# One layer of a Hymba trunk on one core: the sums of a pair of weight tiles made in place, one more buffer of split weights, and one of the pair's sums added by a DMA

## The chip, the cores and the metric

The kernel runs on one core of a Trainium2 chip. The metric is the time of one execution in microseconds of the device. Each time is a median of runs on one chip; a profile comes from one execution of its own. The engines are TensorE (PE; its weight loads are PEld), VectorE (DVE), ScalarE (ACT), GpSimd (POOL) and SyncE (SP); SP and ACT issue plain loads, POOL the DMAs that add.

## The reference, cut to what matters

```
S = 256, D = 2048, F = 5632, float32
x = x + 0.5 * swiglu(rmsnorm(x), wg1, wu1, wd1)      # FFN 1
x = x + mixing(rmsnorm(x))                           # attention and mLSTM heads, projections
x = x + 0.5 * swiglu(rmsnorm(x), wg2, wu2, wd2)      # FFN 2
out = rmsnorm(x)
swiglu(h, wg, wu, wd) = (silu(h @ wg) * (h @ wu)) @ wd
```

The two FFNs make up most of the work: each multiplies 256 rows with two weights of 2048 x 5632 (gate and up) and one of 5632 x 2048 (down), all in float32.

## The kernel before, in words

**Float32 out of three products.** TensorE gets each operand as a high part and a low part. `split` (L112 to L114) makes them: ScalarE casts the source to the high part (L113), VectorE subtracts that from the source for the low part (L114). `mm3` (L139 to L143) then issues three matmuls per product of 128 x 128 by 128 x 512: high by high (L141), high by low (L142), low by high (L143).

**The FFN.** Gate and up have 11 column chunks of 512. They are worked off in parts of 3, 3, 3 and 2 chunks; c = 0, 1, 2 is a chunk's place in its part. After each part the down projection multiplies that part's rows of the hidden state, in two steps of two column chunks each, and its results are scaled on ScalarE (`part`, L281) and added to x by an accumulating DMA from GpSimd (L282). A chunk's gate result goes through Silu on ScalarE (`sg`, L309).

**Paired.** One `Paired` (L322 on) multiplies the activations with two weights at once, `wa` and `wb`: gate and up of a chunk, or two chunks of down. Its first `ns` pairs of k-tiles (4 for gate and up, 2 in one chunk, 3 for down and 1 in the last part) go by a scheme with seven products for eight, out of sums of tiles; the remaining k-tiles go as plain units of two k-tiles each (`plain`). The raw tile of a pair has four rows of 128 x 512: a0 and a1 of wa, b0 and b1 of wb. The sums of weights are T1 = a0 + b0, b0 + b1, T2 = a0 + b0 + b1 and T4 = T2 + a1.

- `first` makes, for each pair, the split tile f (T1 and b0 + b1) and the split tile e (a0 and T2), and multiplies both into the banks p5, p7 (f) and p1, p6 (e) of PSUM. After the split of e, a DMA from GpSimd adds a1 to T2 in the raw tile (L361), which makes T4.
- `combine` mixes the four banks on ScalarE and VectorE (`u`, L368 to L373).
- `second` multiplies the tiles a1 and T4 (`bare`) and b1 (`upper`, two pairs in one split tile), and the plain units of wa. Its results leave two banks, which the caller takes (sg or part).
- `third` multiplies the plain units of wb. It is a generator: `Chain.run` puts its units between the pairs of the next Paired's `first`.

In all 122 pairs are worked off: 82 of gate and up, 40 of down.

**Buffers and order.** The pool `wr` has 4 raw tiles (`raw`), `wrp` has 5 raw buffers of two rows, for plain units (`rawp`) and for the sums (`sums`), `wsp` has 4 split tiles (high `wh`, low `wl`), and PSUM has 6 banks `acc` for products. A buffer is given out in the order in which tiles are asked for, so a split tile waits for the matmuls of the tile four back. The loads, sums and splits of weights are emitted at a priority that is 400 ahead (AHEAD); a scheduler puts the instructions of each engine in a fixed order from these priorities when the program is built, and each engine executes its own in that order. All loads of weights are issued by SP.

In `first` two loads of 512 KB bring a pair's raw tile (L347, issued in L166); VectorE makes T1 and b0 + b1 in a `sums` buffer with one operation of 1024 columns (L350) and T2 in the raw tile with one of 512 (L352); then f and e are split one behind the other.

Of the kernel before, what the change touches and what calls it, by code (L numbers as in the profile page):

```python
# [9 lines left out]
F32 = mybir.dt.float32  # L10
# [3 lines left out]
ALU = mybir.AluOpType  # L14
# [3 lines left out]
P = 128  # L18
# [6 lines left out]
CW = 512  # L25
# [7 lines left out]
UK = 2  # L33
# [4 lines left out]
LK = 4  # L38
AHEAD = 400
# [10 lines left out]
def tile_trunk_layer(ctx: ExitStack, tc: tile.TileContext, x, xt, par, bias_if, lamv, fnorm,  # L50
                     wg1, wu1, wd1, wqk0, wqk1, wqk2, win, wout, wg2, wu2, wd2, out):
    nc = tc.nc
# [2 lines left out]
    slots = ctx.enter_context(tc.tile_pool(name="slots", bufs=21))  # L55
    work = ctx.enter_context(tc.tile_pool(name="work", bufs=8))
    wr = ctx.enter_context(tc.tile_pool(name="wr", bufs=4))
    wrp = ctx.enter_context(tc.tile_pool(name="wrp", bufs=5))
    wsp = ctx.enter_context(tc.tile_pool(name="wsp", bufs=4))
    small = ctx.enter_context(tc.tile_pool(name="small", bufs=2))  # L60
    ps_acc = ctx.enter_context(tc.tile_pool(name="ps_acc", bufs=6, space=PSUM))
    ps_tr = ctx.enter_context(tc.tile_pool(name="ps_tr", bufs=2, space=PSUM))
# [4 lines left out]
    def nm(s):  # L67
        uid[0] += 1
        return f"{s}_{uid[0]}"
# [42 lines left out]
    def split(src, hi, lo):  # L112
        nc.scalar.copy(hi, src)  # L113
        nc.vector.tensor_tensor(out=lo, in0=src, in1=hi.bitcast(F32), op=ALU.subtract)  # L114

    def pair_tiles(pool, tag, shape):
        return (pool.tile(shape, F32R, tag=tag + "h", name=nm(tag + "h")),
                pool.tile(shape, F32R, tag=tag + "l", name=nm(tag + "l")))
# [43 lines left out]
            f()  # L162
        pending.clear()

    def load_pair(dst, w, k):
        nc.sync.dma_start(dst, w[k // LK][:, k % LK:k % LK + 2, :])  # L166

    def load_unit(w, k):
        raw = wrp.tile([P, UK, CW], F32, tag="rawp", name=nm("rawp"))
        with tc.high_priority(offset=AHEAD):  # L170
            load_pair(raw, w, k)
        return raw

    def units(accs, xp, w, nk, last_units=1, ahead=None, in_pieces=False, w0=0,
# [144 lines left out]
    def bank():  # L319
        return ps_acc.tile([P, CW], F32, tag="acc", name=nm("acc"))  # L320

    class Paired:  # L322
# [2 lines left out]

        def __init__(self, xp, wa, wb, nk, ns, w0=0):
            self.xp, self.wa, self.wb, self.k0 = xp, wa, wb, w0 * LK
            self.ns, self.rest = ns, range(2 * ns, nk, UK)  # L330
            self.raws = []

        def prod(self, acc, j, xi, w, wi, first, last, on=False):
            xh, xl = self.xp[j]
            mm3(acc, xh[:, xi, :], xl[:, xi, :], w[0][:, wi, :], w[1][:, wi, :], first, last, on)

        def first(self):


            self.p1, self.p6, self.p7, self.p5 = (bank() for _ in range(4))  # L340
            for j in range(self.ns):
                raw = wr.tile([P, 4, CW], F32, tag="raw", name=nm("raw"))
                self.raws.append(raw)
                at, end = j == 0, j == self.ns - 1
                with tc.high_priority(offset=AHEAD):
                    for i, w in enumerate((self.wa, self.wb)):
                        load_pair(raw[:, 2 * i:2 * i + 2, :], w, self.k0 + 2 * j)  # L347
                    f = pair_tiles(wsp, "w", [P, 2, CW])
                    sums = wrp.tile([P, 2, CW], F32, tag="rawp", name=nm("sums"))
                    nc.vector.tensor_tensor(out=sums, in0=raw[:, 0:4:3, :],  # L350
                                            in1=raw[:, 2:3, :].to_broadcast([P, 2, CW]), op=ALU.add)
                    nc.vector.tensor_tensor(out=raw[:, 2, :], in0=sums[:, 0, :], in1=raw[:, 3, :], op=ALU.add)  # L352
                    e = pair_tiles(wsp, "w", [P, 2, CW])
                    split(sums, *f)
                    split(raw[:, 0:3:2, :], *e)
                self.prod(self.p5, j, S1, f, 0, at, end)
                self.prod(self.p7, j, S3, f, 1, at, end)
                self.prod(self.p1, j, A1, e, 0, at, end)
                self.prod(self.p6, j, S2, e, 1, at, end)
                with tc.high_priority(offset=AHEAD):  # L360
                    nc.gpsimd.dma_start(raw[:, 2, :], raw[:, 1, :], accum_op=ALU.add)  # L361
                yield

        def combine(self):
# [21 lines left out]
        def second(self):  # L386

            n11, n21, n12 = self.p1, self.p7, self.p5

            def bare(j):  # L390
                with tc.high_priority(offset=AHEAD):
                    t = pair_tiles(wsp, "w", [P, 2, CW])
                    split(self.raws[j][:, 1:3, :], *t)
                self.prod(n11, j, A2, t, 0, False, False, True)
                self.prod(n21, j, B2, t, 1, False, False, True)

            def upper(j0):
                with tc.high_priority(offset=AHEAD):
                    t = pair_tiles(wsp, "w", [P, 2, CW])
                    js = range(j0, min(j0 + 2, self.ns))  # L400
                    for i, j in enumerate(js):
                        split(self.raws[j][:, 3, :], t[0][:, i, :], t[1][:, i, :])
                for i, j in enumerate(js):
                    self.prod(n12, j, S4, t, i, False, False, True)

            for i in range(max(self.ns, len(self.rest))):
                if i < self.ns:
                    bare(i)
                    if i % 2 or i == self.ns - 1:
                        upper(i - i % 2)  # L410
                if i < len(self.rest):
                    self.plain(self.wa, self.rest[i], (n11, n21))()
                if i == 0:
                    flush()
            return [n11, n21]
# [46 lines left out]
    def ffn(chain, xp, rstd, wg, wu, wd, finish, first=None):  # L462
# [20 lines left out]
        done = 0  # L483
        for part, (n, ns) in enumerate(zip(PARTS, NP_DOWN)):
            hid = {}
            for c in range(n):
                half, end = inner(hid, c, ns)
                if done + c == 0 and first is not None:
                    half(linear(xp, wg[0], KD, ahead=first[0], in_pieces=True))
                    first[1]()  # L490
                    au = []
                    stream = units(au, xp, wu[0], KD, fine=True)
                    for _ in range(KD // UK - NP):
                        next(stream)
                    first[1]()
                    chain.put(stream, NP, functools.partial(end, au))
                else:
                    np_ = NP
                    if done + c == 1 and first is not None:
                        np_ = NP_FIRST  # L500
                        pending.extend([first[1]] * (NP - NP_FIRST))
                    chain.run(Paired(xp, wg[done + c], wu[done + c], KD, np_), half, end)
            last = part == len(PARTS) - 1
            for c in (0, 2):
                p = Paired(hid, wd[c], wd[c + 1], n * 4, ns, done)
                if last:
                    chain.run(p, functools.partial(finish, c), functools.partial(finish, c + 1),
                              LAST_UNITS if c else 1)
                else:
                    chain.run(p, add(c), add(c + 1))  # L510
            done += n
# [126 lines left out]
    done = 0  # L638
# [385 lines left out]
```

## Time and profile before

| | before |
|---|---|
| median of 3 runs | 1823.52 us (1822.75 to 1824.73) |
| the profiled execution, its own time | 1824.08 us |
| its span | 1822.4 us |
| granted clock of TensorE, mean | 0.998 |
| TensorE busy | 1794.6 us, 98% of the span |
| VectorE busy | 1488.8 us, 82% |
| ScalarE busy | 1121.7 us, 62% |
| GpSimd busy | 156.3 us, 9% |

The span is the profiled execution's stretch on the core; its own time is 1.7 us longer. A group of instructions in the profile is one line of the kernel with an engine, an operation and its tiles: busy time and mean duration, then the idle time of the engine ahead of these instructions and what ended most of it. In a row of the timeline the bracket says how long the engine was idle before the instruction and whose end released it. `L113`, `L114` and `L141` to `L143` are lines of helpers, so the names of the tiles tell which work they belong to: `xt` are plain activations, `xs` sums of activations, `wh` and `wl` split weights.

### The profile page before, as it was taken

The numbers are of one execution on the slowest core, as the hardware profiler recorded it, in microseconds if no ns is written. First come the engines' busy times: TensorE is split into PE (matmuls) and PEld (weight loads), VectorE is DVE, ScalarE is ACT, GpSimd is POOL, SyncE is SP. The second block draws the span as 40 slices with busy tenths as digits, with TensorE's granted clock in tenths as the row PEclk, the third lists the DMA queues.
The fourth block names the chain that finished last, engine by engine and source line by source line (L and its number), as shares of the span: only waits on it lengthen the run. The fifth ranks groups of instructions, "written<-read, shape, count | busy, mean of one in ns | idle before, by whom it ended". The sixth has DMA issues, their size and how long they took to land.

```text
span 1822.4 us, 22684 instructions
## 1 busy us (share of the span) xinstructions
PE 1794.6 (98%) x8090; PEld 1468.2 (81%) x8090; DVE 1488.8 (82%) x1775; ACT 1121.7 (62%) x1443; POOL 156.3 (9%) x199
## 2 busy tenths in 40 slices
PE   8999999999999999999999999999999999999998
PEld 6788788878887888978888888788787888887886
DVE  6889889988998887674465578899889988998886
ACT  6666666666666666554455456666666666666664
POOL 0001100111002100000000000101110021002100
PEclk9999999999999999999999999999999999999999
DMA  8667877797688874553544565677877798678864
GB/s 333 215 204 235 222 234 232 246 250 220 210 252 247 259 237 146 200 185 121 185 159 164 185 213 179 199 228 241 234 230 225 256 247 243 208 230 256 253 190 155
DMA packets 114449, 397.72 MB, mean 218 GB/s; under 512 B 12960, under 2 KB 12960, under 8 KB 107424
## 3 DMA queue, kind: packets, MB, share of 16 engines
q1 hardware_dynamic: 88560, 349.28, 55.5%
q0 software_dynamic: 24480, 44.58, 14.2%
q10 hardware_dynamic: 1296, 2.42, 0.4%
q8 instruction: 63, 1.03, 0.2%
q14 instruction: 50, 0.41, 0.1%
HBM read 349.56 MB, written 2.10 MB: 193 GB/s over the span
## 4 chain that ended last, share of the span: by engine, by line
PE 76%; DMA 9%; DVE 8%; issue 4%; ACT 2%; SPq 1%; POOL 0%; POOLq 0%; DVEq 0%; ACTq 0%
PE acc L142 24%; PE acc L143 24%; PE acc L141 24%; DMA raw<-in_wu_dram 6%; DVE wl L114 5%; ACT wh L113 2%; DVE sums L350 2%; DMA raw<-raw 1%; PE tr L296 1%; SPq L166 1%; DMA xres<-in_x_dram 1%; DVE raw L352 1%; DMA xraw<-in_xt_dram 1%; DMA raw<-in_wd_dram 0%; PE num L808 0%
## 5 line engine op out<-in xcount | busy, mean ns | idle before, releaser
L113 ACT CAST wh<-raw 128x1024 fp32r<-128x1024 f32 (+3 forms) x503 | 464.3, 931 | 377.2 <-PE acc L143 360.9
L114 DVE TENSOR_TENSOR wl<-raw,wh 128x1024 fp32r<-128x1024 f32 (+3 forms) x503 | 535.1, 1074 | 194.7 <-ACT wh L113 191.1
L142 PE MATMUL acc<-wl,xt 128*128 128x512 f32 (+3 forms) x1632 | 630.4, 386 | 4.2 <-DVE wl L114 4.0
L141 PE MATMUL acc<-wh,xt 128*128 128x512 f32 (+3 forms) x1632 | 630.7, 387 | 2.6 <-ACT xt L108 1.5
L143 PE MATMUL acc<-wh,xt 128*128 128x512 f32 (+3 forms) x1632 | 628.8, 386 | 1.2 <-DVE xt L109 1.2
L114 DVE TENSOR_TENSOR wl<-rawp,wh 128x1024 fp32r<-128x1024 f32 x284 | 346.7, 1222 | 43.8 <-ACT wh L113 37.1
L113 ACT CAST wh<-rawp 128x1024 fp32r<-128x1024 f32 x284 | 298.8, 1053 | 117.1 <-PE acc L143 96.4
L141 PE MATMUL acc<-wh,xs 128*128 128x512 f32 x902 | 355.7, 397 | 8.4 <-ACT wh L113 4.0
L142 PEld LDWEIGHTS acc<-wl,xt 128*128 128x128 f32 x1632 | 306.5, 188 | 67.9 <-DVE wl L114 8.8
L141 PEld LDWEIGHTS acc<-wh,xt 128*128 128x128 f32 x1632 | 306.0, 188 | 65.5 <-ACT wh L113 2.8
L143 PEld LDWEIGHTS acc<-wh,xt 128*128 128x128 f32 x1632 | 306.3, 188 | 62.1 <-DVE xt L109 2.5
L142 PE MATMUL acc<-wl,xs 128*128 128x512 f32 x902 | 352.7, 391 | 1.3 <-DVE wl L114 1.1
L143 PE MATMUL acc<-wh,xs 128*128 128x512 f32 x902 | 350.9, 390 | 0.1
L113 ACT CAST wh<-sums 128x1024 fp32r<-128x1024 f32 x122 | 128.4, 1053 | 144.4 <-PE acc L143 139.2
L141 PEld LDWEIGHTS acc<-wh,xs 128*128 128x128 f32 x902 | 169.1, 188 | 57.2 <-ACT u L371 9.3
L142 PEld LDWEIGHTS acc<-wl,xs 128*128 128x128 f32 x902 | 169.4, 188 | 38.9 <-DVE wl L114 6.4
L143 PEld LDWEIGHTS acc<-wh,xs 128*128 128x128 f32 x902 | 169.3, 188 | 36.0 <-DVE xs L109 1.0
L361 POOL DMA_DIRECT2D raw<-raw x122 | 104.0, 853 | 1030.9 <-DVE wl L114 973.7
L350 DVE TENSOR_TENSOR sums<-raw 128x1024 f32<-128x1024 f32 x122 | 149.2, 1223 | 39.4 <-DMA raw<-in_wu_dram 29.2
L114 DVE TENSOR_TENSOR wl<-sums,wh 128x1024 fp32r<-128x1024 f32 x122 | 149.0, 1222 | 14.7 <-ACT wh L113 14.7
L352 DVE TENSOR_TENSOR raw<-sums,raw 128x512 f32<-128x512 f32 x122 | 83.8, 687 | 0.5
L282 POOL DMA_DIRECT2D xres<-part x48 | 43.6, 1060 | 238.2 <-ACT part L281 238.2
(194 smaller groups left out, 756.0 us busy)
## 6 DMA issues: line engine op xcount, KB each, us to landing
rawp<-in_wd_dram SPq DMA_DIRECT2D x96, 512.0 KB, 5.7
rawp<-in_wu_dram SPq DMA_DIRECT2D x94, 512.0 KB, 7.6
raw<-in_wg_dram SPq DMA_DIRECT2D x89, 512.0 KB, 6.7
rawp<-in_wg_dram SPq DMA_DIRECT2D x86, 512.0 KB, 5.7
raw<-in_wu_dram SPq DMA_DIRECT2D x82, 512.0 KB, 7.5
raw<-in_wd_dram SPq DMA_DIRECT2D x80, 512.0 KB, 6.3
raw<-in_win_dram SPq DMA_DIRECT2D x40, 1024.0 KB, 4.8
raw<-raw POOLq DMA_DIRECT2D x122, 256.0 KB, 6.3
```

The costliest lines, as they stand in the source:

```text
L113: nc.scalar.copy(hi, src)
L114: nc.vector.tensor_tensor(out=lo, in0=src, in1=hi.bitcast(F32), op=ALU.subtract)
L141: nc.tensor.matmul(acc, lh, rh, start=first, stop=False, skip_group_check=on)
L142: nc.tensor.matmul(acc, lh, rl, start=False, stop=False, skip_group_check=on)
L143: nc.tensor.matmul(acc, ll, rh, start=False, stop=last, skip_group_check=on)
L166: nc.sync.dma_start(dst, w[k // LK][:, k % LK:k % LK + 2, :])
L282: nc.gpsimd.dma_start(xres[:, hb, c * CW:(c + 1) * CW], t, accum_op=ALU.add)
L296: nc.tensor.transpose(tr[:, i, hb * P:(hb + 1) * P], hs[hb][:, k * P:(k + 1) * P], ident)
L350: nc.vector.tensor_tensor(out=sums, in0=raw[:, 0:4:3, :], in1=raw[:, 2:3, :].to_broadcast([P, 2, CW]), op=ALU.add)
L352: nc.vector.tensor_tensor(out=raw[:, 2, :], in0=sums[:, 0, :], in1=raw[:, 3, :], op=ALU.add)
L361: nc.gpsimd.dma_start(raw[:, 2, :], raw[:, 1, :], accum_op=ALU.add)
```

## The change

- The pool of split tiles gets 5 buffers, the pool of two-row raw buffers 3.
- The sums are made inside the raw tile. At first a0 is loaded into row 3 (256 KB) and b0, b1 into rows 1 and 2 (512 KB). VectorE writes b0 + b1 and T1 over rows 0 and 1 with one operation of 1024 columns (L351 of the new kernel), and f is split from there.
- T2 is made by adding b1 (row 2) onto T1 (row 1) once f is split: for gate and up by an accumulating DMA from GpSimd (L355), but for the last pair of a Paired and for down by VectorE as before (L357).
- e (T2 and a0) is split and multiplied after the next pair's f, not right behind its own.
- a1 is loaded (256 KB) into row 0, which f has left free, after e is emitted, and the DMA that makes T4 (L371) adds it onto T2. `bare` and `upper` read other rows accordingly.
- `first` gives way to the previous `third` at other places: after the first f, then after each e, but for the one that stands between the last two f (with four pairs: after f of pair 0, e of 0, e of 2 and e of 3).

```diff
@@ -55,8 +55,8 @@
     slots = ctx.enter_context(tc.tile_pool(name="slots", bufs=21))
     work = ctx.enter_context(tc.tile_pool(name="work", bufs=8))
     wr = ctx.enter_context(tc.tile_pool(name="wr", bufs=4))
-    wrp = ctx.enter_context(tc.tile_pool(name="wrp", bufs=5))
-    wsp = ctx.enter_context(tc.tile_pool(name="wsp", bufs=4))
+    wrp = ctx.enter_context(tc.tile_pool(name="wrp", bufs=3))
+    wsp = ctx.enter_context(tc.tile_pool(name="wsp", bufs=5))
     small = ctx.enter_context(tc.tile_pool(name="small", bufs=2))
     ps_acc = ctx.enter_context(tc.tile_pool(name="ps_acc", bufs=6, space=PSUM))
     ps_tr = ctx.enter_context(tc.tile_pool(name="ps_tr", bufs=2, space=PSUM))
@@ -162,13 +162,13 @@
             f()
         pending.clear()
 
-    def load_pair(dst, w, k):
-        nc.sync.dma_start(dst, w[k // LK][:, k % LK:k % LK + 2, :])
+    def load_rows(dst, w, k, n):
+        nc.sync.dma_start(dst, w[k // LK][:, k % LK:k % LK + n, :])
 
     def load_unit(w, k):
         raw = wrp.tile([P, UK, CW], F32, tag="rawp", name=nm("rawp"))
         with tc.high_priority(offset=AHEAD):
-            load_pair(raw, w, k)
+            load_rows(raw, w, k, UK)
         return raw
 
     def units(accs, xp, w, nk, last_units=1, ahead=None, in_pieces=False, w0=0,
@@ -325,7 +325,8 @@
 
 
 
-        def __init__(self, xp, wa, wb, nk, ns, w0=0):
+        def __init__(self, xp, wa, wb, nk, ns, w0=0, by_dma=True):
+            self.by_dma = by_dma
             self.xp, self.wa, self.wb, self.k0 = xp, wa, wb, w0 * LK
             self.ns, self.rest = ns, range(2 * ns, nk, UK)
             self.raws = []
@@ -334,31 +335,49 @@
             xh, xl = self.xp[j]
             mm3(acc, xh[:, xi, :], xl[:, xi, :], w[0][:, wi, :], w[1][:, wi, :], first, last, on)
 
         def first(self):
 
             self.p1, self.p6, self.p7, self.p5 = (bank() for _ in range(4))
-            for j in range(self.ns):
+            def f(j):
                 raw = wr.tile([P, 4, CW], F32, tag="raw", name=nm("raw"))
                 self.raws.append(raw)
                 at, end = j == 0, j == self.ns - 1
                 with tc.high_priority(offset=AHEAD):
-                    for i, w in enumerate((self.wa, self.wb)):
-                        load_pair(raw[:, 2 * i:2 * i + 2, :], w, self.k0 + 2 * j)
-                    f = pair_tiles(wsp, "w", [P, 2, CW])
-                    sums = wrp.tile([P, 2, CW], F32, tag="rawp", name=nm("sums"))
-                    nc.vector.tensor_tensor(out=sums, in0=raw[:, 0:4:3, :],
-                                            in1=raw[:, 2:3, :].to_broadcast([P, 2, CW]), op=ALU.add)
-                    nc.vector.tensor_tensor(out=raw[:, 2, :], in0=sums[:, 0, :], in1=raw[:, 3, :], op=ALU.add)
-                    e = pair_tiles(wsp, "w", [P, 2, CW])
-                    split(sums, *f)
-                    split(raw[:, 0:3:2, :], *e)
-                self.prod(self.p5, j, S1, f, 0, at, end)
-                self.prod(self.p7, j, S3, f, 1, at, end)
-                self.prod(self.p1, j, A1, e, 0, at, end)
-                self.prod(self.p6, j, S2, e, 1, at, end)
+                    load_rows(raw[:, 3:4, :], self.wa, self.k0 + 2 * j, 1)
+                    load_rows(raw[:, 1:3, :], self.wb, self.k0 + 2 * j, 2)
+                    t = pair_tiles(wsp, "w", [P, 2, CW])
+                    nc.vector.tensor_tensor(out=raw[:, 0:2, :], in0=raw[:, 2:4, :],
+                                            in1=raw[:, 1:2, :].to_broadcast([P, 2, CW]), op=ALU.add)
+                    split(raw[:, 0:2, :], *t)
+                    if self.by_dma and j < self.ns - 1:
+                        nc.gpsimd.dma_start(raw[:, 1, :], raw[:, 2, :], accum_op=ALU.add)
+                    else:
+                        nc.vector.tensor_tensor(out=raw[:, 1, :], in0=raw[:, 1, :], in1=raw[:, 2, :], op=ALU.add)
+                self.prod(self.p5, j, S1, t, 1, at, end)
+                self.prod(self.p7, j, S3, t, 0, at, end)
+            def e(j):
+                raw = self.raws[j]
+                at, end = j == 0, j == self.ns - 1
                 with tc.high_priority(offset=AHEAD):
-                    nc.gpsimd.dma_start(raw[:, 2, :], raw[:, 1, :], accum_op=ALU.add)
+                    t = pair_tiles(wsp, "w", [P, 2, CW])
+                    split(raw[:, 1:4:2, :], *t)
+                self.prod(self.p1, j, A1, t, 1, at, end)
+                self.prod(self.p6, j, S2, t, 0, at, end)
+                with tc.high_priority(offset=AHEAD):
+                    load_rows(raw[:, 0:1, :], self.wa, self.k0 + 2 * j + 1, 1)
+                    nc.gpsimd.dma_start(raw[:, 1, :], raw[:, 0, :], accum_op=ALU.add)
+            for j in range(self.ns):
+                f(j)
+                if j:
+                    e(j - 1)
+                if j != self.ns - 2:
+                    yield
+            e(self.ns - 1)
+            if self.ns > 1:
                 yield
 
         def combine(self):
@@ -390,7 +409,7 @@
             def bare(j):
                 with tc.high_priority(offset=AHEAD):
                     t = pair_tiles(wsp, "w", [P, 2, CW])
-                    split(self.raws[j][:, 1:3, :], *t)
+                    split(self.raws[j][:, 0:2, :], *t)
                 self.prod(n11, j, A2, t, 0, False, False, True)
                 self.prod(n21, j, B2, t, 1, False, False, True)
 
@@ -399,7 +418,7 @@
                     t = pair_tiles(wsp, "w", [P, 2, CW])
                     js = range(j0, min(j0 + 2, self.ns))
                     for i, j in enumerate(js):
-                        split(self.raws[j][:, 3, :], t[0][:, i, :], t[1][:, i, :])
+                        split(self.raws[j][:, 2, :], t[0][:, i, :], t[1][:, i, :])
                 for i, j in enumerate(js):
                     self.prod(n12, j, S4, t, i, False, False, True)
 
@@ -502,7 +521,7 @@
                     chain.run(Paired(xp, wg[done + c], wu[done + c], KD, np_), half, end)
             last = part == len(PARTS) - 1
             for c in (0, 2):
-                p = Paired(hid, wd[c], wd[c + 1], n * 4, ns, done)
+                p = Paired(hid, wd[c], wd[c + 1], n * 4, ns, done, False)
                 if last:
                     chain.run(p, functools.partial(finish, c), functools.partial(finish, c + 1),
                               LAST_UNITS if c else 1)
```

## The prediction, made before the changed kernel was run

> **What bounds the kernel now.** The page comes first, then windows of 50 us, to see where TensorE is not busy (columns: window, length, busy us of PE, PEld, DVE, ACT, POOL, then clock, DMA share, GB/s).
>
> ```profile
> span 1822.4 us, 22684 instructions
> ...
> PE 1794.6 (98%) x8090; PEld 1468.2 (81%) x8090; DVE 1488.8 (82%) x1775; ACT 1121.7 (62%) x1443; POOL 156.3 (9%) x199
> ```
>
> ```profile
> 0.00:50.00 50.00, 43.09 (x165) 29.59 (x166) 31.00 (x45) 34.30 (x58) 3.65 (x15) 1.00 0.87 317
> ...
> 1800.00:1850.00 50.00, 13.97 (x62) 11.25 (x60) 11.55 (x20) 8.40 (x16) 1.12 (x2) 0.94 0.12 42
> ```
>
> TensorE is the bound. It idles 1822.4 − 1794.6 = 27.8 us: 6.9 in the first window, 22.4 − 14.0 = 8.4 at the end, so 12.5 in the 1750 us between. No matmul is removed: the change can win only such holes, and make new ones. Windows round the starts of gate/up chunks show where they are: first the third chunk of five parts (c=2), then the second chunks (c=1), then the six first chunks behind a down projection (c=0), then the start of the second FFN.
>
> ```profile
> 284.00:304.00 20.00, 19.38 (x86) 15.61 (x85) 17.88 (x21) 13.30 (x16) 2.55 (x3) 1.00 0.80 224
> ...
> sum 100.00, PE 96.80 PEld 77.61 DVE 89.20 ACT 66.06 POOL 12.75; mean PE 19.36 PEld 15.52 DVE 17.84 ACT 13.21 POOL 2.55
> ```
>
> ```profile
> sum 149.00, PE 148.37 PEld 120.39 DVE 136.21 ACT 90.75 POOL 16.13; mean PE 24.73 PEld 20.07 DVE 22.70 ACT 15.13 POOL 2.69
> ```
>
> ```profile
> 380.00:410.00 30.00, 29.18 (x129) 23.76 (x129) 25.06 (x25) 19.37 (x21) 6.14 (x8) 1.00 1.04 291
> ...
> sum 180.00, PE 175.74 PEld 141.22 DVE 152.58 ACT 116.75 POOL 37.79; mean PE 29.29 PEld 23.54 DVE 25.43 ACT 19.46 POOL 6.30
> ```
>
> ```profile
> 1135.00:1165.00 30.00, 28.03 (x119) 21.51 (x118) 25.11 (x29) 17.42 (x19) 4.65 (x5) 1.00 0.71 211
> ```
>
> Holes: 3.2 us at c=2, 0.6 at c=1, 4.3 at c=0, 2.0 at the second FFN. Each stall is longer than its hole, as a matmul is drawn longer than the step between two:
>
> ```profile
> 397.85 0.50 PE L142 MATMUL acc<-wl,xt 128*128 128x512 f32 x1 [0.82 <-DVE wl L114]
> ...
> 400.02 0.39 PE L142 MATMUL acc<-wl,xt 128*128 128x512 f32 x1
> ...
> 400.25 0.39 PE L143 MATMUL acc<-wh,xt 128*128 128x512 f32 x1
> ```
>
> Step 0.23, drawn 0.39: 0.16 more each. That makes 4.0 us at c=2 (five stalls), 1.1 at c=1 (some three), and 4.3 + 10 × 0.16 = 5.9, about 1.0 a chunk, at c=0 (some ten).
>
> **The change part by part.** The view of groups gives the durations, the view of DMA issues the landings (the last two rows: raw<-raw in the window 380 to 410, then in 284 to 304):
>
> ```profile
> L350 DVE TENSOR_TENSOR sums<-raw 128x1024 f32<-128x1024 f32 x122 | 149.2, 1223 | 39.4 <-DMA raw<-in_wu_dram 29.2
> L114 DVE TENSOR_TENSOR wl<-sums,wh 128x1024 fp32r<-128x1024 f32 x122 | 149.0, 1222 | 14.7 <-ACT wh L113 14.7
> L352 DVE TENSOR_TENSOR raw<-sums,raw 128x512 f32<-128x512 f32 x122 | 83.8, 687 | 0.5
> ...
> L113 ACT CAST wh<-sums 128x1024 fp32r<-128x1024 f32 x122 | 128.4, 1053 | 144.4 <-PE acc L143 139.2
> ...
> L361 POOL DMA_DIRECT2D raw<-raw x122 | 104.0, 853 | 1030.9 <-DVE wl L114 973.7
> ...
> L282 POOL DMA_DIRECT2D xres<-part x48 | 43.6, 1060 | 238.2 <-ACT part L281 238.2
> ```
>
> ```profile
> q1 hardware_dynamic: 88560, 349.28, 55.5%
> q0 software_dynamic: 24480, 44.58, 14.2%
> ```
>
> ```profile
> raw<-raw POOLq DMA_DIRECT2D x4, 256.0 KB, 7.0
> ```
>
> ```profile
> raw<-raw POOLq DMA_DIRECT2D x3, 256.0 KB, 5.1
> ```
>
> *Off the path.* 20 chunks × 3 + 1 = 61 T2 additions leave VectorE, 61 × 0.687 = 42 us, and cost POOL 61 × 0.853 = 52 us; neither engine is the bound. q0's 14.2% for 170 transfers (122 and 48) is 1.5 us of all 16 DMA engines each; q1's 55.5% is 0.76 for as many bytes. So 61 more take 93 us, 5 points of the span. The in-place sums cost what L350 costs. 122 more loads are issued on SP: of a pair's three, the third waits for f's split, and stands behind the next pair's loads, so that little is queued behind its wait.
>
> *Fifth split buffer, split loads.* A cast now waits for the tile five back, 6 or 12 matmuls (1.4 or 2.7 us) sooner, and a pair starts on 768 KB, not 1024. I give back half or more of the small stalls that no new wait touches: −0.8 of 1.1 at c=1, −1.0 of some 2.3 at the second FFN (its norm makes the rest), −1.4 of 4.0 at c=2; bounds 0 and −7.4.
>
> The Trainium skill ("DMA: Bandwidth & Descriptors", "Bandwidth") speaks against smaller loads: it wants 1 MiB or more in one DMA. No run here shows 256 KB in a full stream yet.
>
> *The new wait.* e's cast on ScalarE waits for T2, which waits for f's subtraction on VectorE. Both engines are in order. ScalarE at c=0 of part 2 had (f and e of pair 0 are wh_1750 and wh_1755, part the last down's evacuations, which free the PSUM banks of e's two products)
>
> ```order
> L113 CAST wh_351_1750<-sums_353_1752 128x1024
> L113 CAST wh_354_1755<-raw_350_1747 128x1024
> L113 CAST wh_357_1777<-sums_359_1779 128x1024
> L281 ACTIVATE part_344_1737<-acc_289_1480 128x512
> L113 CAST wh_360_1782<-raw_356_1774 128x1024
> L281 ACTIVATE part_345_1740<-acc_291_1482 128x512
> ```
>
> and now has (f wh_1750, f of pair 1 wh_1765, e wh_1777)
>
> ```order
> L113 CAST wh_339_1750<-raw_338_1747 128x1024
> L113 CAST wh_342_1765<-raw_341_1762 128x1024
> L113 CAST wh_344_1777<-raw_338_1747 128x1024
> L113 CAST wh_347_1791<-rawp_346_1789 128x1024
> L113 CAST wh_350_1810<-raw_349_1807 128x1024
> L281 ACTIVATE part_332_1737<-acc_280_1480 128x512
> L113 CAST wh_352_1822<-raw_341_1762 128x1024
> L281 ACTIVATE part_333_1740<-acc_282_1482 128x512
> ```
>
> Part stood behind two casts of early loads; now it stands behind e, a unit and the next f, and its second one behind the next e. On VectorE, f's subtraction wl_1751 stands, as before, behind the sums of pair 2, which wait for loads:
>
> ```order
> L114 TENSOR_TENSOR wl_328_1713<-raw_295_1544,wh_327_1712 128x512
> L351 TENSOR_TENSOR raw_349_1807<-raw_349_1807 128x1024
> L114 TENSOR_TENSOR wl_331_1722<-rawp_329_1719,wh_330_1721 128x1024
> L114 TENSOR_TENSOR wl_340_1751<-raw_338_1747,wh_339_1750 128x1024
> L114 TENSOR_TENSOR wl_343_1766<-raw_341_1762,wh_342_1765 128x1024
> ```
>
> New is that T2 hangs on wl_1751. The same place in the trace of before:
>
> ```profile
> 378.23 0.33 SPq L166 DMA_DIRECT2D raw<-in_wg_dram  x1
> ...
> 383.89 1.05 ACT L113 CAST wh<-rawp 128x1024 fp32r<-128x1024 f32 x1 [0.68 <-PE acc L143]
> ...
> 388.81 1.23 DVE L350 TENSOR_TENSOR sums<-raw 128x1024 f32<-128x1024 f32 x1 [1.61 <-DMA raw<-in_wu_dram]
> ...
> 390.01 0.60 ACT L281 ACTIVATE part<-acc 128x512 f32<-128x512 f32 x1
> ...
> 391.17 0.39 PE L141 MATMUL acc<-wh,xs 128*128 128x512 f32 x1
> ```
>
> The buffer that the unit ahead of f got at 383.85 goes to f itself when there are five. So f is cast at 383.9 and, with no load late, subtracted by 386.1 (1.05 + 1.22 = 2.27). With pair 2's loads in the way it is later. Before, five loads of 512 KB and two evacuations, 5 × 1.52 + 2 × 1.5 = 10.6 us of DMA, went out from 378.2, and the sums began at 378.2 + 10.6 = 388.8. Now three loads' worth is enough, 7.6 us, from some 376.7 (the buffers' last reader stands behind the combine on VectorE, so they gain 1.5, not 2.7): sums at 384.3, and with the unit's and f's subtractions, 3 × 1.22, T2 at 387.9. I take 386.7 for its start, nearer the first, since the loads of all pairs have a lead. It lands at 391.8 with the 5.1 of c=2 (with 7.0: 393.7). Then come on ScalarE e's cast, the unit's, the next f's and part: 3 × 1.05 + 0.60 = 3.75, so 395.6. TensorE wants the bank 12 matmuls (two f) after 391.17: at 393.9. Stall 1.65. The second part stands behind one more cast, 1.65 after the first; TensorE wants it after three matmuls, 0.68: 0.97 more. So 2.6 a chunk against 1.0 now: 6 × 1.6 = +9.6. Bounds: T2 at 386.1 and landing in under 4.1 makes no stall, −5.9; 387.9 and 7.0, 5.7 a chunk, +28.
>
> By the skill's fit for a DMA from GpSimd ("DMA: Bandwidth & Descriptors", "Anatomy of one DMA — SWDGE (gpsimd) path": 2.0 us plus bytes over 436 thousand per us) T2 would land in an estimated 2.6 us, in time at c=0. The traced 5.1 and 7.0 disagree, and they decide.
>
> At c=2 the queue is alike, with the gates sg in the place of part, but units lie between f and e: between what frees f's buffer and what frees e's TensorE does 36 matmuls, 8.2 us, less cast and subtraction 2.27: T2 has 5.9 us against 5.1, so no stall from it (if 2 us late: +10 over five).
>
> *Downs too have e after the next f.* In the last parts' downs, with one pair, e's products follow all third units and combine has less behind it: +0.3 each, +1.2 for four (0 to 4).
>
> Sum: +9.6 − 0.8 − 1.0 − 1.4 + 1.2 = +7.6. The profiled execution took 1824.08, its span plus 1.7, and the median is 1823.52: 1831.7 and 1831.1.
>
> **Rivals.** A measurement of this kernel tells 0.2%, 3.6 us, from no change.
>
> *Faster: T2 lands in time.* It decides whether T2 lands within 4.1 us of 386.1 at c=0. For it: the transfers at c=0 are slow because loads are issued in one burst (share 1.04), and the change moves 256 KB of each pair out of it and starts the rest sooner; VectorE has 0.69 less in each pair. Against: no window above has under 5.1. Then c=0 loses most of 5.9, with the other terms −8: 1815.5; with nearly all holes gone −13.
>
> *No change.* Landing some 1 us late costs c=0 1.3 a chunk, and the rest pays for it: 1823.5. For it: both terms are a fraction of a us in few places.
>
> *Much slower.* The 5 points of DMA share at a share of 1.04 make T2 and loads late together: 5.7 a chunk, 1849. Against: the first phase of a chunk now leaves 4 × 256 KB, 3.0 us of DMA, until after e, against 3 × 1.5 = 4.6 that T2 adds; the burst grows by 1.6 us only.
>
> **How the numbers follow.** Forecast, +4 to +18: 0.38; much slower 0.08; no change 0.20; faster 0.34. So faster 0.34, same 0.20, slower 0.46. Range: low 1812, some 0.08 of the faster case left out; high 1843, the much slower case and a little left out.
>
> **What would show it.** Right: at c=0 behind downs ScalarE's cast waits for raw<-raw, with TensorE's longest holes on part right behind it (some 2 us a chunk); VectorE down by 42 us, POOL up by 52, q0 up by 5 points. Wrong: no such wait there, or raw<-raw landing in 4 us; or new stalls at c=1, c=2 or in the downs.

## The result, and the profile after

The changed kernel takes 1950.35 us, median of four runs (1941.84 to 1956.24), against 1823.66 (1822.75 to 1824.73): ratio 1.069, 95% interval 1.065 to 1.073. It is slower by 127 us. The forecast had the sign but not the size: it said +7.6, with an upper end of 1843.

The page of the kernel after, its first rows and its queues:

```profile
span 1947.8 us, 23123 instructions
...
PE 1838.1 (94%) x8090; PEld 1487.8 (76%) x8090; DVE 1448.5 (74%) x1714; ACT 1107.8 (57%) x1443; POOL 209.7 (11%) x260
...
q1 hardware_dynamic: 106128, 349.29, 53.4%
q0 software_dynamic: 33264, 60.57, 18.6%
```

VectorE is down by 1488.8 − 1448.5 = 40 us, POOL up by 53, q0 up by 4.4 points: what was to leave and to come did so. TensorE's matmuls are the same 8090, yet it is busy 43.5 us longer and idle 110 us rather than 28. Its waits and those of ScalarE say why. From the view of waits (engine, tile and line, what it waited for: us in total, times, longest):

```profile
ACT wh L113 <- PE acc L143: 453.2, 419, 7.1
...
ACT wh L113 <- DMA raw<-raw: 192.0, 38, 9.1
...
DVE raw L351 <- DMA raw<-in_wu_dram: 68.8, 61, 3.3
...
PEld acc L141 <- ACT part L281: 39.9, 12, 6.4
...
PEld acc L141 <- ACT wh L113: 23.0, 16, 3.6
PEld acc L141 <- ACT sg L309: 19.5, 17, 2.2
```

ScalarE waits 38 times, 5 us each, for T2 or T4 to land; 28 of these waits, 163 us, are for T2. In the kernel before it had been 3 in all:

```profile
ACT wh L113 <- DMA raw<-raw: 3.1, 3, 1.5
```

Behind it TensorE waits for the evacuations part and sg and for casts.

The timeline at c=0 of part 1, where the chain can be read step by step (start, duration, engine, line, tile, then the wait ahead of it):

```profile
194.29 1.06 ACT L113 CAST wh<-raw 128x1024 fp32r<-128x1024 f32 x1 [0.26 <-PE acc L143]
...
196.84 1.23 DVE L351 TENSOR_TENSOR raw<-raw 128x1024 f32<-128x1024 f32 x1 [1.48 <-DMA raw<-in_wu_dram]
...
197.99 1.22 DVE L114 TENSOR_TENSOR wl<-rawp,wh 128x1024 fp32r<-128x1024 f32 x1
199.12 2.35 DVE L114 TENSOR_TENSOR wl<-raw,wh 128x1024 fp32r<-128x1024 f32 x2
...
200.63 0.84 POOL L355 DMA_DIRECT2D raw<-raw  x1 [9.19 <-DVE wl L114]
...
207.19 1.04 ACT L113 CAST wh<-raw 128x1024 fp32r<-128x1024 f32 x1 [9.08 <-DMA raw<-raw]
208.14 1.04 ACT L113 CAST wh<-rawp 128x1024 fp32r<-128x1024 f32 x1
...
209.09 1.04 ACT L113 CAST wh<-raw 128x1024 fp32r<-128x1024 f32 x1
...
210.04 0.59 ACT L281 ACTIVATE part<-acc 128x512 f32<-128x512 f32 x1
```

```profile
204.38 0.39 PE L143 MATMUL acc<-wh,xs 128*128 128x512 f32 x1
210.68 0.80 PE L141 MATMUL acc<-wh,xs 128*128 128x512 f32 x1 [5.91 <-ACT part L281]
```

f of pair 0 is cast at 194.29. Its subtraction stands on VectorE behind the sums of pair 2 (196.84, waiting for a load) and the unit's subtraction, so T2 starts at 200.63. By the view of DMA issues it lands 6.5 us later, at 207.1 (its last packet ends some 5.2 us after the start); e's cast starts at 207.19. Two more casts and part follow, and TensorE, due at 204.6, goes on at 210.68. The six chunks behind downs have this stall: 5.91, 5.62, 5.97, 5.31, 5.90, 5.59.

The clock is low behind the stall. Windows of the kernel after, round a stall of 3.0 us at 47 and behind this one (the clock stands ahead of the DMA share):

```profile
46.00:51.00 5.00, 3.32 (x8) 2.20 (x9) 4.61 (x4) 3.30 (x6) 0.90 (x1) 0.66 0.94 298
211.00:215.00 4.00, 4.00 (x10) 2.83 (x10) 3.82 (x4) 1.99 (x3) 3.36 (x4) 0.53 1.00 211
215.00:219.00 4.00, 4.00 (x19) 3.25 (x19) 0.00 (x0) 0.00 (x0) 0.00 (x0) 1.00 1.11 239
```

From 211 to 215 TensorE is busy throughout, but only ten matmuls fall into it, nineteen into the 4 us after that: the granted clock is 0.53, then 1.00.

Adding up what the time between the starts of successive matmuls has over 0.227 gives the account of the 125 us of span: pauses (over 0.3 us more than that) make 119.7 us against 22.3 before (+97; the six at c=0 are 35.3 of it, where the prediction had counted 5.9 for all of c=0), steps between 0.40 and 0.44 us, at half clock, 27.8 against 3.6 (+24), the rest +3. Sorted by the chunk in which they fall, with bounds that may be a few us off, the pauses make 43 us at c=0, 29 at c=1, 24 at c=2 and 13 in the downs, against 5, 5, 5 and under 1 before.

### The profile page after: what moved, and what is told of

Same layout as the page of the kernel before. It is cut to its first block, busy times and chain, and to the rows that moved or that the text cites. A ratio compares the mean times of both kernels' runs of the same rounds, so it can differ in the third digit from the quotient of the medians.

```text
span 1947.8 us, 23123 instructions
## 1 busy us (share of the span) xinstructions
PE 1838.1 (94%) x8090; PEld 1487.8 (76%) x8090; DVE 1448.5 (74%) x1714; ACT 1107.8 (57%) x1443; POOL 209.7 (11%) x260
## 5 line engine op out<-in xcount | busy, mean ns | idle before, releaser
L114 DVE TENSOR_TENSOR wl<-raw,wh 128x1024 fp32r<-128x1024 f32 (+2 forms) x625 | 679.0, 1100 | 336.2 <-ACT wh L113 332.2
L113 ACT CAST wh<-raw 128x1024 fp32r<-128x1024 f32 (+2 forms) x625 | 589.8, 954 | 557.4 <-PE acc L143 300.9
L141 PE MATMUL acc<-wh,xt 128*128 128x512 f32 (+3 forms) x1632 | 638.8, 392 | 5.4 <-ACT wh L113 4.9
L143 PE MATMUL acc<-wh,xt 128*128 128x512 f32 (+3 forms) x1632 | 634.8, 389 | 4.1 <-DVE xt L114 3.9
L141 PE MATMUL acc<-wh,xs 128*128 128x512 f32 x902 | 367.5, 408 | 70.9 <-ACT part L281 34.3
L142 PE MATMUL acc<-wl,xs 128*128 128x512 f32 x902 | 360.1, 399 | 7.0 <-DVE wl L114 6.9
L141 PEld LDWEIGHTS acc<-wh,xt 128*128 128x128 f32 x1632 | 310.9, 191 | 70.3 <-ACT wh L113 7.4
L143 PEld LDWEIGHTS acc<-wh,xt 128*128 128x128 f32 x1632 | 310.1, 190 | 69.9 <-DVE xt L114 6.9
L143 PE MATMUL acc<-wh,xs 128*128 128x512 f32 x902 | 356.7, 397 | 0.1
L351 DVE TENSOR_TENSOR raw<-raw 128x1024 f32<-128x1024 f32 x122 | 149.2, 1223 | 87.8 <-DMA raw<-in_wu_dram 68.8
L371 POOL DMA_DIRECT2D raw<-raw x122 | 108.0, 885 | 633.2 <-DVE wl L114 482.5
L355 POOL DMA_DIRECT2D raw<-raw x61 | 52.3, 858 | 513.0 <-DVE wl L114 400.5
L357 DVE TENSOR_TENSOR raw<-raw 128x512 f32<-128x512 f32 x61 | 41.9, 687 | 0.8
L113 ACT CAST xs<-xsum 128x512 fp32r<-128x512 f32 x28 | 17.2, 618 | 27.9 <-DVE xsum L275 27.9
```

What stands on the lines that cost most here:

```text
L141: nc.tensor.matmul(acc, lh, rh, start=first, stop=False, skip_group_check=on)
L142: nc.tensor.matmul(acc, lh, rl, start=False, stop=False, skip_group_check=on)
L143: nc.tensor.matmul(acc, ll, rh, start=False, stop=last, skip_group_check=on)
L351: nc.vector.tensor_tensor(out=raw[:, 0:2, :], in0=raw[:, 2:4, :], in1=raw[:, 1:2, :].to_broadcast([P, 2, CW]), op=ALU.add)
L355: nc.gpsimd.dma_start(raw[:, 1, :], raw[:, 2, :], accum_op=ALU.add)
L357: nc.vector.tensor_tensor(out=raw[:, 1, :], in0=raw[:, 1, :], in1=raw[:, 2, :], op=ALU.add)
```

## The experiments

Most of them test one theory (A): T2's landing holds e's cast, and with it ScalarE's queue in order, for longer than the split tiles in front of TensorE last. The other letters are rivals of it. The kernels for which one time is given below without an interval were timed once. The four runs of the changed kernel spread over 14 us, so differences of that size between such kernels and it carry little.

**T2 on VectorE everywhere.**

```diff
-                    if self.by_dma and j < self.ns - 1:
+                    if False:
```

> All of the change but for one thing: T2 is added by VectorE in every pair. Theory A (T2's landing of about 5 us holds ScalarE's queue, e's cast first and the evacuations behind it; ScalarE waited 192 us for raw<-raw in the changed kernel): TensorE's stalls over 1 us, 98 us in sum, go, and with them the 25 us of half clock behind them: 1812 to 1826 us. Theory B (e after the next f, the loads in two halves and three rawp buffers are the cause, whoever adds): over 1900 us. Theory C (61 more accumulations load the DMA engines, so that all loads are late): 1812 to 1826 as by A.

1839.69 us, 1.0078 of the kernel before (1.0053 to 1.0103). The DMA is worth 111 of the 127 us. By the same sorting the pauses are 3, 3 and 7 us at c=0, 1 and 2, as short as before the change or nearly so, and 19 in the downs. Theory B falls, but 14 to 16 us stay that A did not expect. TensorE waits there on the activations' sums in the first down of a part, as it does in the changed kernel (11.9 us) and hardly in the kernel before:

```profile
PEld acc L141 <- ACT xs L113: 13.7, 8, 2.5
```

```profile
PEld acc L141 <- ACT xs L113: 0.3, 1, 0.3
```

VectorE's wait for loads ahead of the sums (68.8 us in the changed kernel) is 67.9 here: it does not come from T2's DMAs, and it is not what cost the 111 us.

**The DMA without the wait.**

```diff
+    idle = const.tile([P, CW], F32, name="idle")
+    nc.gpsimd.memset(idle, 0.0)
...
-                    if self.by_dma and j < self.ns - 1:
-                        nc.gpsimd.dma_start(raw[:, 1, :], raw[:, 2, :], accum_op=ALU.add)
-                    else:
-                        nc.vector.tensor_tensor(out=raw[:, 1, :], in0=raw[:, 1, :], in1=raw[:, 2, :], op=ALU.add)
+                    nc.vector.tensor_tensor(out=raw[:, 1, :], in0=raw[:, 1, :], in1=raw[:, 2, :], op=ALU.add)
+                    if self.by_dma and j < self.ns - 1:
+                        nc.gpsimd.dma_start(idle, raw[:, 2, :], accum_op=ALU.add)
```

> As the kernel with T2 on VectorE everywhere, and in the pairs in which the change adds T2 by DMA the same DMA is issued beside it, b1 added onto a scratch tile that nothing reads. Theory A (waiting for the landing): within 6 us of the kernel without these DMAs, since nobody waits for them. Theory C (DMA load): most of the 126 us come back, over 1880 us.

1848.32 us, 9 over the kernel without these DMAs; a little more than A allowed. Its q0 carries as much as that of the changed kernel:

```profile
q0 software_dynamic: 33264, 60.57, 19.4%
```

So the load of 61 more accumulations is some 9 us by this one run, and the waiting the other hundred. Theory C falls. The idle DMAs wait for each other, as all add onto one tile, so they do not go out just when T2's would.

**Evacuations first.**

```diff
-        nc.scalar.activation(t, acc, AF.Copy, scale=0.5)
+        with soon():
+            nc.scalar.activation(t, acc, AF.Copy, scale=0.5)
...
-        nc.scalar.activation(s, src, AF.Silu, scale=r)
+        with soon():
+            nc.scalar.activation(s, src, AF.Silu, scale=r)
```

(`soon` is a helper of the kernel that raises the priority further, by 40 over that of the weights.)

> The changed kernel with the evacuations part and sg at a higher priority: in ScalarE's order the first part of a chunk behind a down stands right behind e's cast, no longer behind the unit's and the next f's casts. Theory A: the six stalls of 5.3 to 6.0 us at c=0 shrink by two casts, 2.1 us, to about 3.6, and the time by 13 to 25 us, to 1925 to 1937 us. Theories B and C (loads late): the six stalls stay over 5 us, 1945 to 1955 us.

1964.99 us: a miss. The six stalls did shrink, to 4.19, 3.93, 3.75, 2.90, 2.58 and 3.36, mean 3.45 as A had it, but the time was 15 us over the changed kernel's median and 9 over its slowest run. TensorE in this kernel at the first of these chunks, two rows with what lies between left out:

```profile
209.37 0.50 PE L141 MATMUL acc<-wh,xs 128*128 128x512 f32 x1 [4.19 <-ACT part L282]
```

```profile
223.24 0.51 PE L141 MATMUL acc<-wh,xs 128*128 128x512 f32 x1 [3.22 <-ACT wh L113]
```

What the first pair no longer waited for, the third pair's e waited for, 14 us on: in these chunks 0.95 to 3.22 us each time. That fits the evacuation being where the wait shows, not what it is made of.

**Only the buffers, in the kernel before.**

```diff
-    wrp = ctx.enter_context(tc.tile_pool(name="wrp", bufs=5))
-    wsp = ctx.enter_context(tc.tile_pool(name="wsp", bufs=4))
+    wrp = ctx.enter_context(tc.tile_pool(name="wrp", bufs=3))
+    wsp = ctx.enter_context(tc.tile_pool(name="wsp", bufs=5))
```

> The kernel before with nothing changed but the buffers: five of split weights and three of rawp (which hold the sums too). Theory A (the fifth buffer gives loads and casts a lead and the prediction's gain at c=0, c=1, c=2 and the second FFN was right): 1815 to 1821 us. Rival D (three rawp buffers, shared with the sums, hold back the loads of plain units): 1826 us or more, with casts of rawp waiting for their loads.

1827.56 us, ratio 1.0009 (0.9997 to 1.0021): no difference that can be measured. The casts now wait for loads of plain units, for which the kernel before waited 0.3 us in all:

```profile
ACT wh L113 <- DMA rawp<-in_wd_dram: 47.8, 30, 3.0
ACT wh L113 <- DMA rawp<-in_wu_dram: 40.3, 19, 5.5
```

So the lead of the fifth tile seems spent on the two raw buffers that are missing. In this kernel the three buffers hold the sums too, which the changed kernel keeps in the raw tile, so the run is harder on them than the change is.

**How far e stands from f.** Three distances, with T2 by DMA in all: e right behind its f; e behind the next f (the change); e behind the f after next, in chunks of four pairs alone and for the first two pairs alone.

```diff
             for j in range(self.ns):
                 f(j)
-                if j:
-                    e(j - 1)
-                if j != self.ns - 2:
-                    yield
-            e(self.ns - 1)
-            if self.ns > 1:
-                yield
+                e(j)
+                yield
```

> The changed kernel, but e is emitted right behind its own f, as the kernel before has it: no other f stands between T2's start and e's cast. Theory A (ScalarE's queue waits until T2 has landed, about 6.5 us from issue to the cast, and five split tiles cover some 8 us of TensorE): all 61 waits show, some 5 us each, +150 to +350 us over the changed kernel, 2100 to 2300 us. Theory A' (only the evacuations behind e's cast matter, at c=0 and c=2): about as the changed kernel, 1930 to 1990 us.

```diff
+            if self.by_dma and self.ns == 4:
+                f(0)
+                yield
+                f(1)
+                yield
+                f(2)
+                e(0)
+                yield
+                f(3)
+                e(1)
+                e(2)
+                e(3)
+                yield
+                return
```

> The changed kernel, but with four pairs e is emitted after the f of two pairs on (f0, unit, f1, unit, f2, e0, unit, f3, e1, e2, e3, unit): T2 has one or two tiles more to land in. Theory A: the waits for raw<-raw on ScalarE, 192 us in 38, fall below 40 us, the six stalls at c=0 go, and the time comes down to that of T2 on VectorE with the idle DMAs, 1840 to 1865 us. Theory A': the evacuations still stand behind e, over 1920 us.

2189.38, 1950 and 1843.69 us; the first and the last lie within A's figures. The units between the pairs move along with e, and at distance 0 the downs have the old order too; nothing else is changed. ScalarE's wait for the landing, first at distance 0, then at distance 2:

```profile
ACT wh L113 <- DMA raw<-raw: 367.1, 59, 12.0
```

```profile
ACT wh L113 <- DMA raw<-raw: 109.7, 52, 6.6
```

At distance 2 it still waits 110 us in all (A had said below 40), and at c=0 e's cast is no earlier than in the changed kernel, 207.29 against 207.19 (ScalarE, part 1):

```profile
201.33 0.60 ACT L281 ACTIVATE part<-acc 128x512 f32<-128x512 f32 x1 [0.54 <-PE acc L143]
207.29 1.05 ACT L113 CAST wh<-raw 128x1024 fp32r<-128x1024 f32 x1 [5.36 <-DMA raw<-raw]
```

But part and the unit's cast are ahead of it now, TensorE has work, and of the six stalls none is left over 0.5 us on part. This bears A out: a wait costs only what outlasts the work in front of TensorE.

**The first pair by VectorE.**

```diff
-                    if self.by_dma and j < self.ns - 1:
+                    if self.by_dma and 0 < j < self.ns - 1:
```

> The changed kernel, but T2 of a chunk's first pair is added by VectorE too: 40 accumulating DMAs stay of 61. Theory A: the six stalls of 5.3 to 6.0 us at c=0, 34 us, hang on the first pair's T2 and go, with some 10 us of the half clock behind them; the waits of the second and third pairs stay: 1885 to 1915 us. Rival E (each chunk waits for one landing, whichever pair it is, as e3 showed for the evacuations): the wait moves to the next pair, 1925 us or more.

1917.84 us: 32 less, between the two theories' figures, nearer to A's upper end. The six stalls on part are gone, but in their place, one pair on, stand 5.37, 3.97, 4.34, 3.19, 5.41 and 5.40 us:

```profile
217.47 0.80 PE L141 MATMUL acc<-wh,xs 128*128 128x512 f32 x1 [5.37 <-ACT wh L113]
```

So rival E seems to have the mechanism right (a chunk waits for one long landing, whichever pair has it), and the time that fewer DMAs save must come from other waits.

**The in-place sums alone.** T2 on VectorE as in the first experiment, and e right behind f as in the kernel before.

> T2 on VectorE in every pair and e right behind its own f: of the change only the in-place sums, the split loads and the five and three buffers are left. The kernel with T2 on VectorE and e after the next f took 1839.7, 16 us over the kernel before. If that is the order of e (its products and the combine come later, and downs with one pair lose their cover): 1820 to 1830 us. If it is the in-place sums (T2 is written over T1 and so must wait for f's cast and subtraction): 1836 us or more.

1915.51 us, 1.0495 (1.0466 to 1.0524). In place T2 overwrites T1, so it has to wait until f is cast and subtracted, whoever adds it; e's cast waits for that:

```profile
ACT wh L113 <- DVE raw L357: 241.4, 68, 10.3
```

The kernel before made T2 from a buffer of its own ahead of both splits. The sums in place, with the split loads and the five and three buffers, cost some 90 us while e stays in its old place; no run parts them. e after the next f buys back 76 of them, and the kernel with T2 on VectorE is then still 15 us behind.

**Where e has room, the old way elsewhere.** Gate and up with four pairs go f0, unit, f1, unit, f2, e0, f3, e1, unit, e2, e3, unit with T2 by DMA as the change has it; down and the chunk with two pairs as before the change. The second kernel has T2 on VectorE besides.

```diff
-            for j in range(self.ns):
-                f(j)
-                if j:
-                    e(j - 1)
...
+            if not self.by_dma or self.ns != 4:
+                self.o = 1
+                for j in range(self.ns):
+                    both(j)
+                    yield
+                return
+            f(0)
+            yield
+            f(1)
+            yield
+            f(2)
+            e(0)
+            f(3)
+            e(1)
+            yield
+            e(2)
+            e(3)
+            yield
```

(`both` is the old loop's body with sums in a rawp buffer; `self.o` is the first row that `bare` reads.)

> Gate and up with four pairs keep the change with T2 by DMA, in the order f0, unit, f1, unit, f2, e0, f3, e1, unit, e2, e3, unit; down and the chunk with two pairs are made as in the kernel before (sums in a rawp buffer, e right behind f). The kernel with e two later took 1843.7; its stalls over 1 us stood on the sums of activations in the downs (xs 9.3, xt 4.6 us), on the first chunk (3.1) and on the combine (u 6.5). Theory A (only what e's cast has to wait out counts): these 17 us and more go, 1815 to 1828 us. Rival F (the 61 accumulations cost by their DMA load, +9 in the run with idle DMAs): 1832 us or more.

> As the hybrid, but T2 on VectorE in all pairs. Theory A: with e two f later neither way of adding T2 is waited for, so the two differ by VectorE's 42 us of relief against 93 us of DMA time, both off the path: within 6 us of the hybrid. If VectorE's relief pays: over 6 us slower than the hybrid. If the DMAs' load costs as in the run with idle DMAs: some 9 us faster.

With T2 by DMA 1835.98 us, 1.0054 (1.0036 to 1.0071); with T2 on VectorE 1823.51, 0.9988 (0.9974 to 1.0003). Rival F is borne out: 12 us for the DMAs, near the 9 of the idle ones, though ScalarE's wait for them (first kernel 113 us, second 2) is in it too and the runs do not part the two:

```profile
ACT wh L113 <- DMA raw<-raw: 113.3, 48, 5.8
```

```profile
ACT wh L113 <- DMA raw<-raw: 2.1, 3, 1.2
```

VectorE's relief, 1447.9 us busy against 1482.4, bought nothing that shows beside that. The best version is no faster than the kernel before by a measurement.

**Four split buffers in the changed kernel.**

```diff
-    wrp = ctx.enter_context(tc.tile_pool(name="wrp", bufs=3))
-    wsp = ctx.enter_context(tc.tile_pool(name="wsp", bufs=5))
+    wrp = ctx.enter_context(tc.tile_pool(name="wrp", bufs=5))
+    wsp = ctx.enter_context(tc.tile_pool(name="wsp", bufs=4))
```

> The changed kernel with four buffers of split weights and five of rawp, as before the change. Theory A: each of the 38 waits for T2 has one tile of 6 or 12 matmuls (1.4 or 2.7 us) less in front of TensorE, and waits that five tiles hid come out: +55 to +120 us over the changed kernel, 2000 to 2070 us. If the ring has no part in it: 1945 to 1960 us.

1968.84 us, +18, 13 over the changed kernel's slowest run: a miss, a third of the least that A had. The order of ScalarE was made anew and differs, so the wait is not the old one plus a tile, and two raw buffers more came with the smaller ring; how they share is open.

**An eighth of T2's bytes.**

```diff
-                        nc.gpsimd.dma_start(raw[:, 1, :], raw[:, 2, :], accum_op=ALU.add)
+                        nc.gpsimd.dma_start(raw[:, 1, 0:64], raw[:, 2, 0:64], accum_op=ALU.add)
```

> The changed kernel, but T2's DMA adds 64 of the 512 columns (32 KB, not 256), so that the other 448 columns of T2 are left out of the result. If the wait is mostly the transfer itself and its share of the full DMA engines: raw<-raw of L355 lands in about 2 us, the waits go, 1840 to 1865 us. If it is mostly what every such DMA takes (issue 0.86 us, first packet 1.4 to 4 us after the issue's start, release of the waiting cast 0.5 to 1.3 us after the last packet, as the changed kernel's trace has it): landing 3 to 4.5 us, half or more of the loss stays, 1880 to 1930 us.

1897.43 us: 53 less, 74 of the loss stay. The kernel leaves out seven eighths of the addition, so only its time counts. The last packet of these 32 KB comes 3.7 us after their issue (median of 61), that of the 256 KB of the changed kernel 5.3; to the landing in the view of DMA issues it is 4.3 and 6.2. (The scheduler also put the next f behind part in ScalarE's order here, one cast of 1.05 us less ahead of it.) At the first of the chunks behind downs T2 starts 199.02 and e is cast at

```profile
203.39 1.04 ACT L113 CAST wh<-raw 128x1024 fp32r<-128x1024 f32 x1 [6.99 <-DMA raw<-raw]
```

4.4 us after the start for an eighth of the bytes, 6.6 for all. Seven eighths of the bytes are worth 2.2 us, so by an estimate all of them are worth 2.5 of the 6.6: most of a landing is not the transfer.

## Why the prediction was wrong, point by point

**The bound, and what left VectorE and came to POOL and the queues:** right, to within 2 us and 0.6 points.

**"The new wait" at c=0:** the chain was right in every link (T2 behind f's subtraction, that behind the sums of pair 2, then e, unit, next f, part), the sizes were not. Counted from f's cast, T2 started 6.3 us on, where 2.8 was taken and 4.0 was the late bound: the loads ahead of the sums came late. It landed in 6.5 against 5.1, by the same view. From e's cast to TensorE's next matmul, three casts and part, it took 3.5 against 3.75. Together 16.4 against 11.7, with the cast 0.1 behind the landing, and a stall of 5.7 on the first part alone, where 1.65 was taken (2.6 with the second part). That the price of "much slower" at c=0 is the same number, 5.7, is in part chance: it was for two parts, with T2 landing in 7.0.

**The step that failed by most: "T2 has 5.9 us against 5.1, so no stall from it", at c=2, and that second chunks only gain.** The 5.1 was the median of three landings of T4 in one window; over all 122 of them the page of the kernel before has

```profile
raw<-raw POOLq DMA_DIRECT2D x122, 256.0 KB, 6.3
```

and the 61 T2 of the changed kernel took, by the same measure (line L355),

```profile
DMA to landing us min/median/max: 4.4/6.2/8.4
```

So 33 of the 61 outlast the cover of 5.9 even where it is as long as was taken. A cast of e that waits also makes the next f and its T2 late; that waits follow each other through a chunk in this way fits the two runs that moved a wait (evacuations first, first pair by VectorE), but was not counted. Beside the 35.3 − 5.9 = 29 us of the six stalls TensorE's pauses grew by 97 − 29 = 68 us: some 24 at c=1, 19 at c=2 and 13 in the downs, the rest mostly later in the first chunks. With T2 on VectorE those at c=1 and c=2 go, all but 2 us at c=2, and those in the downs stay. New stalls at c=1, c=2 or in the downs were what the prediction had named as its sign of being wrong.

**The clock:** no term for it. 24 us went to steps at half clock, in stretches of 2 to 5 us each, each behind pauses of some 2 us or more (one, or two close together). The Trainium skill ("TensorE: Matmul & The Clock Gate", "Part 1: The HAM clock gate") has the clock fall to half after an idle window of about 3.4 us and come back after as long a busy one. The trace agrees in kind, with steps of 0.42 for 0.227 us and low stretches in its clock record of 3.4 or 6.8 us, though some of its pauses are shorter, and some pairs of pauses of 1.0 to 1.4 us have no such stretch behind them. That the pauses bring it about is read from the order of the two in the trace; no run tried it by itself.

**"Fifth split buffer, split loads: −3.2":** no gain shows. The buffers alone, in the kernel before, measured 1.0009, with new waits for the loads of plain units where two raw buffers were missing; the change had been given no price for these two. In the changed kernel, four and five buffers were 18 us slower in one run, so there the fifth may be worth something. The split loads were not tried alone.

**"Downs too": +1.2, at most 4.** Too small: with T2 on VectorE the change was 15 us behind, and with the old way in the downs and the two-pair chunk (and another order in gate and up) that was gone. The waits were on the activations' sums (xs), not on the combine.

**The in-place sums, "cost what L350 costs":** true of the operation, not of the order it forces. T2 could no longer be made ahead of f's split. That was seen for the DMA and not weighed for VectorE.

**The other price for T2's landing:** the Trainium skill's fit of 2.0 us plus bytes over 436 thousand ("DMA: Bandwidth & Descriptors", "Anatomy of one DMA — SWDGE (gpsimd) path") gives an estimated 2.6 us for 256 KB and 2.1 for 32 KB; traced were 5.3 and 3.7 to the last packet, 6.2 and 4.3 to the landing. It has the right shape, a fixed part with less for the bytes, and would have kept T2 in time, which the trace does not bear out. The prediction was right to go by the traced landings; it took too short a one.

## What to carry to other kernels

A DMA in place of a 0.7 us addition is a latency in place of a duration: price it from its issue to the start of the instruction behind it (here 6.6 us, of which the bytes are somewhat over a third by the estimate above), by the landings of all such transfers and not by the shortest window, and count what stands between its producer and its consumer in tiles that the bound engine still has in front of it. An operation made in place can take away an order as well as a buffer. And a wait on an engine in order need not go when the instruction that showed it is moved; here it showed at the next one.

## What the runs showed of the hardware that was not expected

What comes behind TensorE's pauses: from before to after the half clock takes 24 us, though the mean clock only falls from 0.998 to 0.975. With e right behind f it takes 79 us, at a mean of 0.933.

The accumulating DMA of 32 KB took 70% of the time of the one of 256 KB (3.7 against 5.3 us to the last packet). In the changed kernel the cast that waited for one of 256 KB started some 0.5 us or more after its last packet, 0.9 in the median of the 38 waits.
